# Finer hand placement in a two-layer attention trunk: score steps merged, gates and contraction quarters reordered, key transposes moved

## The chip, the cores and the metric

One core of one Trainium2 chip runs the whole kernel. The metric is the device time of one execution in microseconds (us), compared as the median of several runs. Engines are named as in the profile: PE (TensorE matmul), PEld (its weight loads), DVE (VectorE), ACT (ScalarE), POOL (GpSimd), SP (the queue that issues most DMAs).

## The reference, cut to what matters

Two residual layers work on 256 tokens of width 2048, with a memory of 256 tokens. A head is 128 wide, and all arithmetic is float32.

```
mem_n = rms_norm(mem)
for i in range(2):
    h = rms_norm(x)
    proj = h @ (even_w_in | odd_w_in)                # 2048 x 6680 | 2048 x 6224
    # even: 8 "nsa" heads: compressed + selected-block + window branches, sigmoid gates
    #       4 "diff" heads: softmax_1 - lam * softmax_2, then rms_norm
    #       4 memory heads over mem_n @ mem_w_kv
    # odd : 12 "dsa" heads: an indexer scores the keys, the top 64 of them are attended
    #       4 memory heads
    y = concat(heads) * silu(gate columns of proj)   # 2048 wide: 16 tiles of 128
    x = x + y @ w_out[i]
```

## The kernel before

**Products.** A weight matrix is cut into chunks (the list `CHUNKS`, line 32), and a chunk into pieces of 512 KB or less. Line 174 loads a piece into a ring of four buffers. Lines 185 and 186 split it into a high part `whi` (ACT) and a rest `wlo` (DVE), up to two pieces ahead of the product. Two kinds of product use the pieces. `dense_nat` (line 262) gives tokens by columns in twelve matmuls of 512 columns per piece (24 narrower ones for a narrow chunk). `dense_T` (lines 277 and 278) gives columns by tokens in sixteen matmuls per piece, eight of 512 and eight of 256 columns; it makes the gates (chunks z0 to z7 in the even layer, y0 to y7 in the odd one) and the out projections (o0 to o7, p0 to p7). A gate chunk has four pieces. The products write PSUM tiles named `dn`, of which there are two.

**Order of the chunks.** Keys and values of the memory for both layers (memk0, memv0, memk1, memv1), then the even layer: mq0, cmp0, cmp1, bq, bk, bv, ks, vs0, vs1, aq0, aq1, z0 to z7, o0 to o7; then the odd layer: ikw, iq0, iq1, mq11, ck, cv, cq0 to cq2, y0 to y7, p0 to p7.

**Attention as steps.** Each head is a Python generator; its `yield`s cut it into steps. `attend` (line 211) queues a head. At most two heads are open at once (`lines`), and `step` (line 217) advances them in turn. After each piece, `run_background` lets `PER_PIECE` = 0.9 of a step run; `attended` forces steps until the named heads are over. Steps are traced with high priority. A planner that simulates the engines then sets the order of each engine's queue, so a step may stand later on the chip than where it was traced. Each engine works through its queue in that order.

**Steps of one head.** An nsa head (line 974) has five: scores and softmax of token block 0; the same of block 1; rescaling and the first branch's transposes and split; the second branch's; then the product with the values (lines 1003 to 1005). A diff head (line 842) has four. A dsa head (line 1188) and a memory head (line 543) have three, and both blocks' scores go into one PSUM tile: block 0's matmuls, its softmax, block 1's matmuls, its softmax. Scores, transposes and value products share three PSUM buffers.

**Gate and head meet in `Gated`** (line 422). Each of the 16 tiles of y has two factors. Whichever comes first is stored in `oT` (a head by one ACT copy, line 439; a gate by lines 1029 and 1030), the second is multiplied in (a head by one DVE operation, line 440; a gate by lines 1033 and 1034). When a pair of tiles is complete and its quarter released, `flush` splits it into `y` (lines 286 and 287), which the out projection reads. The quarters hold: 0 and 1 the nsa heads 0 to 3 and 4 to 7, 2 the diff heads, 3 the memory heads; in the odd layer 0 to 2 the dsa heads, 3 the memory heads. A quarter of `y` takes the place of tiles that the heads still read, so the even layer releases 2 and 3 when the diff heads are over and 0 and 1 after all nsa heads; the odd layer releases all four at the end.

**Memory keys.** `mem_k` (line 519) copies memk's product into a tile `nat` (two buffers, shared with its squares), has POOL compute the reciprocal norms by small operations one after the other (`rsq`, lines 301 to 314), multiplies (line 525, DVE), and transposes four heads for each token block on PE (line 354, through the single PSUM buffer `pp`). The transposes are traced right behind the multiplication. While memk0's keys wait for the norms, PE works on memv0 and memk1; for memk1's keys it works on memv1.

Of the kernel before, what the change touches and what calls it, by code (L numbers as in the profile page):

```python
# [33 lines left out]
for _i, _c in enumerate((2584, 2840, 3096, 3352, 5144, 5400, 6168, 6424)):  # L34
    CHUNKS.append((f"z{_i}", "even", _c, 256))
# [5 lines left out]
for _i, _c in enumerate((3664, 3920, 4176, 4432, 4688, 4944, 5712, 5968)):  # L41
    CHUNKS.append((f"y{_i}", "odd", _c, 256))
# [7 lines left out]

OFFS = {}
# [5 lines left out]
NCOLS = {c[0]: c[3] for c in CHUNKS}  # L57

# [57 lines left out]
def trunk(tc, xT, memT, W, w1, w2, consts, ctab, grow, gcol, outT):  # L116
    nc = tc.nc
    V, A, T, G = nc.vector, nc.scalar, nc.tensor, nc.gpsimd
    with ExitStack() as ctx:
# [42 lines left out]
        PER_PIECE = 0.9  # L162
# [88 lines left out]
        def dense_nat(act, name):  # L251
# [4 lines left out]
            for q in range(KT // k):  # L256
                wh, wl = weights(first[name] + q)
                for k_ in range(k):
                    kt = q * k + k_
                    for j, (part, w) in enumerate(((0, wh), (1, wh), (0, wl))):  # L260
                        for tb in range(2):
                            T.matmul(ps[:, tb, :n], act[kt, part, tb * P:(tb + 1) * P], w[:, k_, :],  # L262
                                     start=(kt == 0 and j == 0), stop=(kt == KT - 1 and j == 2), skip_group_check=True)
# [3 lines left out]
        def dense_T(act, name, apart=False):  # L267
# [3 lines left out]
            for q in range(4):  # L271
                wh, wl = weights(first[name] + q)
                for n in range(8):
                    ct, k_ = (n // 4, n % 4) if apart and q == 3 else (n % 2, n // 2)
                    kt = q * 4 + k_
                    cs = slice(ct * P, (ct + 1) * P)
                    T.matmul(ps[:, ct, :], wh[:, k_, cs], act.both(kt), start=(kt == 0), stop=False, skip_group_check=True)  # L277
                    T.matmul(ps[:, ct, S:], wl[:, k_, cs], act[kt, 0, :], start=False, stop=(kt == KT - 1),  # L278
# [143 lines left out]
        class Gated:  # L422
# [3 lines left out]
            def __init__(self, oT, act):  # L426
                self.oT, self.act, self.seen, self.ready, self.free = oT, act, set(), set(), set()

# [90 lines left out]
        def mem_k(v, rm, done):  # L519
# [6 lines left out]
            for tb in range(2):  # L526
                done(tb, transpose4(kn[:, tb], 4, prep_bank()))
# [15 lines left out]
        def mem_attention(q, nsc, qi, h, kT, v, out, obase):  # L543
# [109 lines left out]
        mem_k(dense_nat(memA, "memk1"), rm, spill_k)  # L653
# [55 lines left out]
        out = Gated(big.tile([P, KT, S], F32, name="oT0", tag="S0"), y)  # L709
# [132 lines left out]
        def diff_head(h, q, nsd, bkT, bv, ob):  # L842
            E = tp.tile([P, 2, 3 * P], F32, name="E")
            sm = sp.tile([P, 2, 2], F32, name="sm")
            for tb in range(2):
# [7 lines left out]
                yield  # L853
# [66 lines left out]
        for g in range(2):  # L920
# [3 lines left out]
            if g == 0:  # L924
# [374 lines left out]
```

## Time and profile before

| | us |
|---|---|
| median of 3 runs | 972.97 |
| the runs | 972.97, 973.02, 970.55 |
| the profiled execution | 969.85 |
| its span in the trace | 968.1 |
| PE / PEld / DVE / ACT / POOL busy | 950.3 / 807.5 / 669.6 / 516.8 / 130.1 |

The profiled execution is a run of its own; its span begins with the first instruction and ends with the last. Matmuls are pipelined and their ends are modelled, so PE's busy time runs past the start of the next matmul: 98% busy does not say that PE worked at its full pace, but an idle PE in the trace is idle.

### The profile page before, as it was taken

Reading aid. Unit: us, or ns where it says so; the run is one execution under the profiler, and the core shown is the slowest. Engines: PE = TensorE matmul, PEld = TensorE weight load, DVE = VectorE, ACT = ScalarE, POOL = GpSimd, SP = SyncE. Lnnn points to the kernel's source line nnn. Section 1 sums busy time; section 2 is a strip of 40 time slices with the busy share of each in tenths; the row PEclk is TensorE's granted clock in tenths of the full one; section 3 lists DMA queues with packets and bytes.
Section 4 is the critical chain, followed back from the end, with each engine's and each line's share of the span. In section 5 each row is a group of like instructions: output and inputs, shape, how many; then the busy total and the mean of one; then the engine's idle time right before and its main releaser. Section 6 shows DMA issues by size and latency. Waiting matters only on the chain.

```text
span 968.1 us, 14359 instructions
## 1 busy us (share of the span) xinstructions
PE 950.3 (98%) x5225; PEld 807.5 (83%) x5225; DVE 669.6 (69%) x1137; ACT 516.8 (53%) x853; POOL 130.1 (13%) x345
## 2 busy tenths in 40 slices
PE   8989999999999999999899999999999999999998
PEld 6878788777787888888788898888888888888886
DVE  6768866655665677777776676779766676677553
ACT  6656544545555546666555454555545566564332
POOL 0073120320211220000000131021023020000000
PEclk9999999999999999999999999999999999999999
DMA  9756755757476655344488775544555455546772
GB/s 331 246 194 196 240 187 175 235 188 233 131 264 190 187 168 154 123 140 144 139 257 249 208 236 182 169 132 139 178 187 175 159 170 164 164 131 193 241 236 89
DMA packets 55623, 182.06 MB, mean 188 GB/s; under 512 B 6352, under 2 KB 7888, under 8 KB 55552
## 3 DMA queue, kind: packets, MB, share of 16 engines
q1 hardware_dynamic: 53904, 176.77, 57.4%
q0 software_dynamic: 1216, 4.05, 1.4%
q8 instruction: 41, 0.67, 0.3%
q10 hardware_dynamic: 432, 0.32, 0.1%
q14 instruction: 30, 0.25, 0.1%
HBM read 175.88 MB, written 5.24 MB: 187 GB/s over the span
## 4 chain that ended last, share of the span: by engine, by line
PE 89%; DVE 4%; POOL 2%; DMA 2%; issue 1%; ACT 1%; SPq 0%; ACTq 0%; DVEq 0%; POOLq 0%
PE dn L262 41%; PE dn L277 25%; PE dn L278 13%; DVE wlo L186 1%; PE pp L354 1%; PE S L747 1%; DMA raw<-in_W 1%; PE pt L354 1%; PE S L1131 1%; PE S L983 1%; PE po L1003 1%; PE po L567 1%; ACT whi L185 1%; PE S L550 1%; DMA xs<-in_xT 1%
## 5 line engine op out<-in xcount | busy, mean ns | idle before, releaser
L186 DVE TENSOR_TENSOR wlo<-raw,whi 128x1024 fp32r<-128x1024 f32 (+3 forms) x305 | 364.3, 1196 | 199.3 <-ACT whi L185 196.3
L185 ACT ACTIVATE whi<-raw 128x1024 fp32r<-128x1024 f32 (+3 forms) x305 | 316.5, 1039 | 311.4 <-PE dn L262 129.5
L262 PE MATMUL dn<-whi,h 128*128 128x512 f32 (+3 forms) x1152 | 295.7, 372 | 0.0
L262 PEld LDWEIGHTS dn<-whi,h 128*128 128x128 f32 x1152 | 203.9, 188 | 38.1 <-issue 4.3
L277 PE MATMUL dn<-h,whi 128*128 128x512 f32 x576 | 206.9, 398 | 1.8 <-DVE rp L460 1.8
L277 PE MATMUL dn<-y,whi 128*128 128x512 f32 x512 | 179.7, 397 | 2.2 <-DVE y L287 2.2
L262 PE MATMUL dn<-wlo,h 128*128 128x512 f32 (+3 forms) x576 | 169.5, 373 | 0.0
L278 PE MATMUL dn<-h,wlo 128*128 128x256 f32 x576 | 163.7, 284 | 0.0
L278 PE MATMUL dn<-y,wlo 128*128 128x256 f32 x512 | 142.8, 279 | 0.0
L277 PEld LDWEIGHTS dn<-h,whi 128*128 128x128 f32 x576 | 108.2, 188 | 24.9 <-DVE rp L460 2.2
L262 PEld LDWEIGHTS dn<-wlo,h 128*128 128x128 f32 x576 | 103.4, 188 | 18.6 <-issue 1.6
L277 PEld LDWEIGHTS dn<-y,whi 128*128 128x128 f32 x512 | 96.0, 188 | 25.7 <-DVE y L287 2.7
L278 PEld LDWEIGHTS dn<-h,wlo 128*128 128x128 f32 x576 | 108.8, 189 | 0.7
L278 PEld LDWEIGHTS dn<-y,wlo 128*128 128x128 f32 x512 | 96.4, 188 | 0.1
L262 PE MATMUL dn<-whi,mem 128*128 128x512 f32 x256 | 71.1, 398 | 1.7 <-ACT mem L485 1.2
L262 PEld LDWEIGHTS dn<-whi,mem 128*128 128x128 f32 x256 | 48.5, 191 | 13.7 <-ACT mem L485 2.4
L383 ACT ACTIVATE E<-E,mn 128x128 f32<-128x128 f32 (+1 forms) x88 | 40.2, 457 | 31.3 <-DVE mn L382 24.3
L262 PE MATMUL dn<-wlo,mem 128*128 128x512 f32 x128 | 40.5, 397 | 0.4 <-DVE wlo L186 0.4
L1062 POOL DMA_DIRECT2D x1d<-x x8 | 4.4, 550 | 199.1 <-DVE x L1059 188.1
L262 PEld LDWEIGHTS dn<-wlo,mem 128*128 128x128 f32 x128 | 24.2, 190 | 5.7 <-DVE wlo L186 0.6
L286 ACT ACTIVATE prh<-pt 128x384 fp32r<-128x384 f32 (+2 forms) x36 | 16.8, 473 | 15.2 <-PE pt L354 10.9
L313 POOL TENSOR_SCALAR rsa<-rsa 128x8 f32<-128x8 f32 (+4 forms) x57 | 22.6, 397 | 5.0
(331 smaller groups left out, 967.5 us busy)
## 6 DMA issues: line engine op xcount, KB each, us to landing
raw<-in_W SPq DMA_DIRECT2D x287, 512.0 KB, 3.9
raw<-in_w SPq DMA_DIRECT2D x16, 512.0 KB, 4.4
raw<-in_W SPq DMA_DIRECT2D x8, 336.0 KB, 3.6
raw<-in_W SPq DMA_DIRECT2D x8, 280.0 KB, 3.1
xs<-in_xT SPq DMA_DIRECT2D x8, 256.0 KB, 6.3
ld<-in_xT SPq DMA_DIRECT2D x8, 256.0 KB, 3.6
x1d<-x POOLq DMA_DIRECT2D x8, 256.0 KB, 4.1
ld<-x1d SPq DMA_DIRECT2D x8, 256.0 KB, 3.8
```

The lines of the kernel that those rows point to most:

```text
L185: state["last"] = (A.activation(hi[:, c], r[:, c], AF.Copy), V.tensor_tensor(lo[:, c], r[:, c], hi[:, c].bitcast(F32), OP.subtract))
L186: V.tensor_tensor(lo[:, c], r[:, c], hi[:, c].bitcast(F32), OP.subtract))
L262: T.matmul(ps[:, tb, :n], act[kt, part, tb * P:(tb + 1) * P], w[:, k_, :], start=(kt == 0 and j == 0), stop=(kt == KT - 1 and j == 2), ski ...
L277: T.matmul(ps[:, ct, :], wh[:, k_, cs], act.both(kt), start=(kt == 0), stop=False, skip_group_check=True)
L278: T.matmul(ps[:, ct, S:], wl[:, k_, cs], act[kt, 0, :], start=False, stop=(kt == KT - 1), skip_group_check=True)
L286: A.activation(hi, src, AF.Copy)
L313: G.tensor_scalar(a, a, 1.5, None, OP.add)
L354: T.transpose(ps[:, b, :], src[:, b * P:(b + 1) * P], ident)
L383: A.activation(E, E, AF.Exp, bias=mn, scale=-1.0, accum_out=sm)
L550: T.matmul(ps_s[:, tb, :], a[:, qi, block(tb)], b[:, h, :], start=(j == 0), stop=(j == 2))
L567: T.matmul(po, a[:, mt, h * P:(h + 1) * P], b[:, mt, :], start=(mt == 0 and j == 0), stop=(mt == 1 and j == 2))
L747: T.matmul(ph[l4 * 32:(l4 + 1) * 32, :], blks[j][:, l, :, :].rearrange("p g c -> p (g c)"), wt[:, l4, :], start=(l < 4), stop=(l >= 28), t ...
```

## The change

- Chunks: aq0 goes ahead of vs1. The gates go in the orders `ORDER0` = 3, 2, 1, 0, 4, 5, 6, 7 and `ORDER1` = 5, 4, 3, 0, 1, 2, 6, 7.
- `K_ORDER`: the even layer's out projection contracts the quarters in the order 2, 0, 1, 3; its weights are packed in that order.
- Steps: `PER_PIECE` is 1.2. A diff or nsa head issues the scores of both token blocks in one step (four steps for an nsa head, three for a diff head). A memory head issues both blocks' score matmuls before the first softmax; a dsa head issues block 1's, then block 0's, then the softmaxes in that order.
- A head named in `behind` (even: 2 to 7; odd: 6 to 11) yields ahead of its value product until its gate has been stored.
- `mem_k`'s transposes become a background generator that yields 15 times (memk0) or 5 times (memk1), once per piece, and then queues them behind the last product matmul traced so far.

```diff
-          ("vs0", "even", ((1792, 128), (2304, 128), (2560, 24)), 280), ("vs1", "even", ((1920, 128), (2432, 128)), 256),
-          ("aq0", "even", 0, 512), ("aq1", "even", 512, 512)]
+          ("vs0", "even", ((1792, 128), (2304, 128), (2560, 24)), 280), ("aq0", "even", 0, 512),
+          ("vs1", "even", ((1920, 128), (2432, 128)), 256), ("aq1", "even", 512, 512)]
+ORDER0 = (3, 2, 1, 0, 4, 5, 6, 7)
+ORDER1 = (5, 4, 3, 0, 1, 2, 6, 7)
+K_ORDER = {"out0": (2, 0, 1, 3)}
...
-        PER_PIECE = 0.9
+        PER_PIECE = 1.2
+        MEM_LATER = 15
...
-            for q in range(4):
+            for q, quarter in enumerate(K_ORDER.get(SOURCE[name], range(4))):
...
-                    kt = q * 4 + k_
+                    kt = quarter * 4 + k_
...
+            def waits(self, c):
+
+                return c in self.behind and c not in self.seen
...
-            for tb in range(2):
-                done(tb, transpose4(kn[:, tb], 4, prep_bank()))
+
+            def transposes():
+
+                for _ in range(MEM_LATER):
+                    yield
+                with tc.issue_after(state["product"].ins):
+                    for tb in range(2):
+                        done(tb, transpose4(kn[:, tb], 4, prep_bank()))
+
+            start_background(transposes(), 1)
...
                 for j, (a, b) in enumerate(passes(q, kT)):
                     T.matmul(ps_s[:, tb, :], a[:, qi, block(tb)], b[:, h, :], start=(j == 0), stop=(j == 2))
+            for tb in range(2):
                 softmax_masked(ps_s[:, tb, :], None, nsc[:, tb, qi:qi + 1], E[:, tb, :], sm[:, tb:tb + 1])
...
-        mem_k(dense_nat(memA, "memk1"), rm, spill_k)
+        v = dense_nat(memA, "memk1")
+        MEM_LATER = 5
+        mem_k(v, rm, spill_k)
...
-                yield
+            yield
             V.reciprocal(sm, sm)
             V.tensor_tensor(sm, sm, gate4[:, :, h, 1:3], OP.mult)
...
-            while compressed not in over:
+            while compressed not in over or out.waits(h):
                 yield
...
-        for i in range(8):
+        for i in ORDER0:
             gated(out, f"z{i}", i * 2, h0)
...
+            for j, (a, b) in enumerate(passes(q1, kT)):
+                T.matmul(ps_s[:, 1, :], a[:, qi, :], b[:, g, :], start=(j == 0), stop=(j == 2))
+            T.matmul(ps_s[:, 0, :P], q0[:, qi, :], k0[:, g, :], start=True, stop=True)
+            for tb in (1, 0):
+                softmax_masked(ps_s[:, tb, :(tb + 1) * P], biases[tb], nsc[:, tb, qi:qi + 1], E[:, part(tb)], sm[:, tb:tb + 1])
```

## Rows read from the trace of the kernel before

**Rows 1.** The page: busy time of PE (share of the span, instructions), and the granted clock of PE in 40 equal slices, in tenths.
```profile
PE 950.3 (98%) x5225; PEld 807.5 (83%) x5225; DVE 669.6 (69%) x1137; ACT 516.8 (53%) x853; POOL 130.1 (13%) x345
...
PEclk9999999999999999999999999999999999999999
```

**Rows 2.** The waits of PE's weight loads over the whole span: what waited <- for what: us in total, times, longest.
```profile
PEld pp L354 <- DVE nat L525: 3.1, 1, 3.1
PEld dn L277 <- DVE y L287: 2.7, 2, 1.5
PEld dn L277 <- DVE rp L460: 2.2, 2, 1.3
PEld pt L354 <- DVE prl L287: 2.0, 1, 2.0
...
PEld S L1198 <- DVE mn L382: 1.1, 1, 1.1
...
PEld po L1003 <- DVE prl L287: 0.8, 1, 0.8
```

**Rows 3.** The timeline of PE around 66 us: start, us, instruction, in brackets the idle time before it and what ended it.
```profile
62.49 0.84 PE L262 MATMUL dn<-whi,mem 128*128 128x512 f32 x3
65.99 0.66 PE L354 MATMUL pp<-cst,nat 128*128 128x128 f32 x4 [2.65 <-DVE nat L525]
...
67.29 1.91 PE L262 MATMUL dn<-whi,mem 128*128 128x512 f32 x4
```

**Rows 4.** Two stretches of 20 us: busy us (and instructions) of PE, PEld, DVE, ACT, POOL, then the granted clock, the DMA share and GB/s.
```profile
40.00:60.00 20.00, 20.00 (x94) 16.71 (x93) 14.02 (x25) 10.74 (x16) 7.91 (x21) 1.00 0.82 276
60.00:80.00 20.00, 17.34 (x74) 13.88 (x74) 13.28 (x18) 9.36 (x15) 10.66 (x32) 0.91 0.55 174
```

**Rows 5.** The timeline of POOL, first for memk0's keys (59 to 65 us), then for memk1's (86 to 96 us).
```profile
58.98 0.20 POOL L301 TENSOR_TENSOR ssq<-ssq,rmk 128x8 f32<-128x8 f32 x1
...
64.48 0.20 POOL L301 TENSOR_TENSOR mkf<-mkf,rmk 128x8 f32<-128x8 f32 x1
...
86.30 3.64 POOL L301 TENSOR_TENSOR ssq<-ssq,rmk 128x8 f32<-128x8 f32 x1 [13.27 <-DVE ssq L323]
...
95.84 0.20 POOL L301 TENSOR_TENSOR mkf<-mkf,rmk 128x8 f32<-128x8 f32 x1
```

**Rows 6.** The timeline of all engines around memk1's keys: the copy of the product, DVE work beside POOL, the multiplication, the first transposes.
```profile
81.36 1.01 ACT L522 ACTIVATE nat<-dn 128x1024 f32<-128x1024 f32 x1
...
86.52 1.22 DVE L186 TENSOR_TENSOR wlo<-raw,whi 128x1024 fp32r<-128x1024 f32 x1
...
96.08 1.22 DVE L525 TENSOR_TENSOR nat<-nat,mkf 128x1024 f32<-128x1024 f32 x1 [3.88 <-POOL mkf L301]
...
97.83 0.60 PE L354 MATMUL pp<-cst,nat 128*128 128x128 f32 x4
```

**Rows 7.** The timeline of PE at the end of the even layer's attention. Reading `h` is the last gate, reading `y` the out projection.
```profile
460.80 0.28 PE L278 MATMUL dn<-h,wlo 128*128 128x256 f32 x1
460.92 0.39 PE L277 MATMUL dn<-y,whi 128*128 128x512 f32 x1
...
463.69 1.15 PE L354 MATMUL pt<-cst,E 128*128 128x128 f32 x9
466.61 0.55 PE L354 MATMUL pt<-cst,E 128*128 128x128 f32 x3 [1.77 <-DVE prl L287]
467.68 0.39 PE L1003 MATMUL po<-prh,vv 128*128 128x256 f32 x1 [0.52 <-DVE prl L287]
...
472.22 0.50 PE L277 MATMUL dn<-y,whi 128*128 128x512 f32 x1 [1.28 <-DVE y L287]
```

**Rows 8.** The timeline of PE inside the even layer's gates (389 us) and at the end of the odd layer's attention (858 to 874 us).
```profile
388.90 0.50 PE L277 MATMUL dn<-h,whi 128*128 128x512 f32 x1 [0.72 <-DVE rp L460]
...
858.22 0.62 PE L1198 MATMUL S<-kT,qh 128*128 128x256 f32 x3 [0.86 <-DVE mn L382]
859.96 0.50 PE L277 MATMUL dn<-h,whi 128*128 128x512 f32 x1 [1.11 <-DVE rp L460]
...
874.19 0.50 PE L277 MATMUL dn<-y,whi 128*128 128x512 f32 x1 [0.90 <-DVE y L287]
```

**Rows 9.** The end of the even layer's gates as one stretch, 26 us (columns as in rows 4): all instructions, and below it only those that write or read `dn`.
```profile
435.00:461.00 26.00, 26.00 (x164) 23.21 (x163) 20.39 (x45) 17.91 (x39) 0.00 (x0) 1.00 0.46 142
...
435.00:461.00 26.00, 21.38 (x114) 17.15 (x113) 0.86 (x2) 0.59 (x1) 1.00 0.46 142
```

**Rows 10.** Groups of DVE instructions by line over the span: busy us, mean ns of one | idle before.
```profile
L186 DVE TENSOR_TENSOR wlo<-raw,whi 128x1024 fp32r<-128x1024 f32 (+3 forms) x305 | 364.3, 1196 | 199.3 <-ACT whi L185 196.3 <-PE dn L262 2.2
...
L460 DVE TENSOR_TENSOR rp<-rp,dn 128x512 f32<-128x512 f32 x16 | 10.9, 678 | 0.9 <-ACT rp L459 0.7
L287 DVE TENSOR_TENSOR y<-oT,y 128x512 fp32r<-128x512 f32 x16 | 10.5, 684 | 0.4 <-ACT y L286 0.3
...
L1034 DVE SCALAR_TENSOR_TENSOR oT<-ew,rp 128x512 f32<-128x512 f32 (+1 forms) x12 | 8.0, 664 | 0.2
```

**Rows 11.** Groups of ACT instructions of a gate (columns as in rows 10).
```profile
L1026 ACT ACTIVATE ew<-rp 128x512 f32<-128x512 f32 x16 | 9.9, 621 | 3.7 <-DVE rp L460 3.5 <-DVE rp L1024 0.3
L286 ACT ACTIVATE y<-oT 128x512 fp32r<-128x512 f32 x16 | 9.4, 620 | 2.6 <-PE po L1004 1.5 <-DVE oT L1034 1.0
L459 ACT ACTIVATE rp<-dn 128x512 f32<-128x512 f32 x16 | 9.3, 583 | 1.1 <-DVE oT L1030 1.0
```

More of the change, by code (lines that the diff above doesn't have):

```diff
@@ L57 @@
 NCOLS = {c[0]: c[3] for c in CHUNKS}
+SOURCE = {c[0]: c[1] for c in CHUNKS}
 CC = {}
@@ L261, in dense_nat @@
                         for tb in range(2):
-                            T.matmul(ps[:, tb, :n], act[kt, part, tb * P:(tb + 1) * P], w[:, k_, :],
-                                     start=(kt == 0 and j == 0), stop=(kt == KT - 1 and j == 2), skip_group_check=True)
+                            state["product"] = T.matmul(
+                                ps[:, tb, :n], act[kt, part, tb * P:(tb + 1) * P], w[:, k_, :],
+                                start=(kt == 0 and j == 0), stop=(kt == KT - 1 and j == 2), skip_group_check=True)
                 run_background()
@@ L708, in trunk @@
         y = Act("B", "y0", False)
-        out = Gated(big.tile([P, KT, S], F32, name="oT0", tag="S0"), y)
+        out = Gated(big.tile([P, KT, S], F32, name="oT0", tag="S0"), y, range(2, 8))
         r = region("B", 0, "kT", F32R)
@@ L919, in trunk, with values @@
             split(*[x.rearrange("p g b s -> p (g b) s")[:, :, block(tb)] for x in kT], transpose4(kn[:, tb], 4, prep_bank()))
-        for g in range(2):
+        def values(g):
             w = dense_nat(h0, f"vs{g}")
@@ L1084, in trunk @@
         y = Act("B", "y1", False)
-        out = Gated(big.tile([P, KT, S], F32, name="oT1", tag="S0"), y)
+        out = Gated(big.tile([P, KT, S], F32, name="oT1", tag="S0"), y, range(6, 12))
         r = region("B", 0, "kv1")
@@ L1191, in dsa_head @@
             ps_s = pS.tile([P, 2, S], F32, name="S", tag="one")
-            for tb in range(2):
-                n = (tb + 1) * P
-                if tb == 0:
-                    T.matmul(ps_s[:, 0, :P], q0[:, qi, :], k0[:, g, :], start=True, stop=True)
-                else:
-                    for j, (a, b) in enumerate(passes(q1, kT)):
-                        T.matmul(ps_s[:, 1, :], a[:, qi, :], b[:, g, :], start=(j == 0), stop=(j == 2))
-                softmax_masked(ps_s[:, tb, :n], biases[tb], nsc[:, tb, qi:qi + 1], E[:, part(tb)], sm[:, tb:tb + 1])
+            for j, (a, b) in enumerate(passes(q1, kT)):
[3 more added lines that the diff above has]
+                softmax_masked(ps_s[:, tb, :(tb + 1) * P], biases[tb], nsc[:, tb, qi:qi + 1], E[:, part(tb)], sm[:, tb:tb + 1])
             V.reciprocal(sm, sm)
@@ L1210, in dsa_head @@
             yield
+            while out.waits(h):
+                yield
             vg = slice(g * P, (g + 1) * P)
@@ L1231, in trunk @@
             dsa += [attend(dsa_head(c * 4 + i, q0, q1, nsc), *chosen) for i in range(4)]
-        for i in range(8):
+        for i in ORDER1:
             gated(out, f"y{i}", i * 2, h1, rb1)
```

28 lines of the change are left out of this document (18 added, 10 removed).

## The prediction, made before the changed kernel had run

> **What bounds the kernel now.** I read the page first. PE is busy for 950.3 of 968.1 us at a granted clock of 9 tenths or more in every slice [rows 1]; no other engine passes 69%. Since a busy PE need not be at its pace, the question is how long PE stood still. The waits answer it. Those of the weight loads, which stand at the head of PE's queue, come to 3.1 + 2.7 + 2.2 + 2.0 + 1.1 + 0.8 = 11.9 us in eight waits that belong to lines of the change [rows 2]. The timeline of PE then shows where they lie: one ahead of the transposes of memk0's keys [rows 3], one inside the even layer's gates, three at the end of the even layer's attention [rows 7], and three at the end of the odd layer's [rows 8].
>
> The first costs more than its wait. In the stretch from 60 to 80 us the granted clock is 0.91, and PE starts 74 instructions instead of 94 in the stretch before [rows 4]. The 20 that are missing, at 20/94 = 0.21 us each, are 4.3 us: the wait of 2.65 us and 1.6 us of matmuls at half the clock (1.2 instead of 2.4 GHz). The same shows directly: three matmuls took 0.84 us ahead of the wait, four took 1.91 us behind it [rows 3].
>
> So the most that this change can win is 3.1 + 1.6 for memk0's keys and 11.9 - 3.1 = 8.8 for the others, 13.5 us. It takes no matmul away. Whatever else it does can only move work off or onto PE's waits.
>
> **Memory transposes later.** A background generator yields once per piece, so with 15 yields memk0's transposes are queued at the 16th piece counted from memv0's first: behind memk1's last. Before they stood at 66 us, in memk1's fourth piece, the twelfth in that count [rows 3]; four pieces more at about 2.77 us (a piece of sixteen matmuls runs from 460.92 to 463.69 [rows 7], and one of twelve moves as many columns) give 11 us. The keys are ready at once when DVE's multiplication ends, ahead of 66 us [rows 3], so the wait and the slow matmuls go: **-4.7 us**. Late next on that spot is DVE's `wlo`, queued behind the multiplication that waits for POOL; it works two pieces ahead, 5.5 us, so I price it at 0, at most 0.7.
>
> For memk1's keys the margin is thin. Before, the copy of the product began at 81.36 and the multiplied keys were there at 96.08 + 1.22 = 97.30, 15.9 us later; PE took them at 97.83 without a wait [rows 6]. In the changed kernel the transposes may not stand ahead of the end of memv1's sixth piece, 6 x 2.77 = 16.6 us behind memk1. That alone fits. But `nat` has two buffers: memk1's copy needs the one that memk0's keys leave, and those are now transposed only behind memk1. With one `pp` buffer that takes four transposes (0.66 us [rows 3]), a split on ACT and DVE (0.62 and 0.68, by the split of y [rows 10, 11]), and four more transposes: 2.6 us. The keys are then ready about 18.5 us behind memk1, against 16.6. If the planner foresees it, it places the transposes a piece later and nothing is lost; if not, PE waits 1.9 us, up to the 2.7 us that the reading of 16.7 + 2.6 gives, and pays the slow clock as memk0's did. Behind that copy ACT's `whi` for memv1 is queued; two pieces of lead, 5.5 us, cover 2.6. Between 0 and 2.7 + 1.6 = 4.3 I take **+0.7**, near the row without a wait [rows 6], since the planner placed these keys well before.
>
> POOL is the uncertain part of this chain. The same first operation took 0.20 us for memk0's keys and 3.64 for memk1's, where DVE ran `wlo` beside it [rows 5, 6]; the whole chain took 5.7 us (58.98 to 64.68) and 9.7 us (86.30 to 96.04). The Trainium skill says the same on its page GPSIMD Engine Reference, section 8 (Key points): POOL shares its SBUF interfaces with VectorE, in contention with DVE instructions that have two SBUF inputs. By that rule the later place of memk1's chain is not a safer one, and the thin margin above is a rival, priced below; these rows agree with the rule.
>
> **Steps, merged scores, the pace.** I counted the steps by the code. Before, 0.9 per piece and five steps for an nsa head leave eight steps of heads 6 and 7 undone when the last gate's product ends; PE meets their transposes and value products behind the out projection's first piece, at 463.69, and waits there [rows 7]. With 1.2 per piece and four steps a head takes 3.33 pieces instead of 5.56. Heads 2 and 3 hold both places until z1, the third gate, is stored; the steps in between do nothing, and no engine waits for a generator that yields. Then twenty pieces of gates remain, and the heads 4 to 7 with their compressed branch need (4 x 4 + 2) / 1.2 = 15. The last value product falls to z7's first piece, three pieces (8.3 us) ahead of the gates' end. In the odd layer the heads 8 to 11 need 4 x 3 / 1.2 = 10 of the last twenty pieces. So the transposes and value products that PE waited for (2.0 + 0.8 us), the scores behind a softmax in the same tile (1.1; block 1's matmuls no longer stand behind block 0's softmax), and y of the even layer (1.5 of the 2.7) all go: **-5.4 us**.
>
> The quarters' order gives the out projection one more piece of cover: quarter 2 is ready long before, and quarter 3, which needs the last gate, comes last. That gate's chain is 0.58 + 0.68 + 0.62 + 2 x 0.66 + 0.62 + 0.68 = 4.5 us [rows 10, 11], under the 8.3 us of the three pieces ahead. In the odd layer the order stays 0 to 3; the heads end earlier, so of its wait for y (1.2 us with the load's, 0.90 in rows 8) I let 0.4 stay: **-0.8**. Gates first or heads first changes which engine stores, by some tenths on ACT and DVE, hidden behind PE: 0. aq0 ahead of vs1 moves the same instructions: 0, with one wait as in rows 8 (1.1) as its bound on either side.
>
> **What the denser steps cost.** At the end of the gates, 26 us hold 114 matmuls of products, 7.1 pieces, and 20.39 us of DVE [rows 9]: per piece 3.66 us of time and 2.87 of DVE. Of that `wlo` is 1.20 and a gate's share (0.68 + 2 x 0.66 + 0.68)/4 = 0.67 [rows 10], which leaves 1.00 for the heads; PE's own work for them is 3.66 - 2.77 = 0.89. A head in 3.33 instead of 5.56 pieces makes both 1.67 times as dense: DVE 1.87 + 1.67 = 3.54 us in 2.77 + 1.49 = 4.26, or 83% instead of 78%. It holds on the mean, but bunches can delay a gate's `total` (line 460), for which the product after next waits for its `dn` tile. Such waits were two, 2.2 us together [rows 2, 8]. The old two go where the bunches were (-2.2); for new ones I take **+1.5**, between 0 and 6 (one in every third of the sixteen gates at 1.1).
>
> **The sum.** -4.7 + 0.7 - 5.4 - 0.8 - 2.2 + 1.5 = -10.9 us, say -11. The profiled execution took 969.85 us, of which 968.1 are its span; the median of the runs is 972.97, 3.1 us above it. The waits should be the same in all of them, so I subtract from the median: **962.0 us**. From the profiled execution it would be 958.9.
>
> **Rivals.**
> - *The wait moves to memk1's keys.* For it: the two-buffer `nat`, POOL's 9.7 us. Against it: PE did not wait there before. The price is 4.3 instead of 0.7, so -7.3: 965.7 us. Chance 0.17.
> - *The heads still end behind the gates* (the change doesn't do what it says). Steps are only traced early; the planner and the engines can lag. For it: before, the odd layer's last step was traced in y6, and its scores stood at 858 us, the seventh gate's end [rows 8]. Against it: three pieces of slack in the even layer, nine in the odd. If the even layer's three waits and the odd layer's y stay, 4.3 + 0.8 less is won: -5.9, 967.1 us. Chance 0.13.
> - *Slower: DVE falls behind the gates.* If the denser heads make every gate's `total` late, sixteen gates wait 1.1 us as at 859.96 [rows 8]: +17.6 instead of +1.5, so +5: 978 us. It beats the gain from about eleven gates on. For it: DVE's 83% and its place at the end of most of the waits in rows 2. Against it: only two such waits at 78%. Chance 0.07.
> - *Two of the first two together*: -2.3, 970.7 us. Chance 0.03.
>
> **How the numbers follow.** The forecast has 0.60 and, with the bounds of its terms (no new wait: -13.5, 959.5; six new waits in the gates: -6.4) and the 2.5 us over which the runs scatter, spans 958 to 967. The range 957.5 to 969.5 takes in the first two rivals and leaves out slower and the pair. What counts as no change here is 0.3%, 2.9 us, so faster means below 970.05. That holds for nearly all of the forecast and both first rivals, less the scatter: faster 0.83; same 0.10 (the pair, and rivals meeting a slow set of runs); slower 0.07.
>
> **What would show it.** In the profile after: no wait ahead of `pp` at 63 to 66 us and a granted clock of 1.00 in 60 to 80; memk1's `pp` behind memv1's sixth piece, waiting 0 to 0.7; the last value product of either layer ahead of its last gate's end; no weight load waiting for `prl`; the sum of the listed waits about 2 to 3 us instead of 11.9. The prediction is wrong if PE waits for line 460 in many gates, if memk1's `pp` waits over 2 us with a clock below 1 behind it, or if the out projections' first pieces still wait for y.

## The result and the profile after

The changed kernel takes **958.27 us** (median of four runs, 957.76 to 958.86) beside 972.42 for the kernel before in the same session (four runs, 970.55 to 973.02): ratio 0.9858, 95% interval 0.9841 to 0.9875, or 14.2 us less. The forecast was 962.0 with a range of 957.5 to 969.5, so the time lies inside the range and 3.7 us below the forecast. The profiled execution took 957.76 us, its span 956.0, which is 12.1 us less than the span of before.

I read the page first. PE is as near to the whole span as it was, and its busy time has fallen from 950.3 to 945.0 us with the same 5225 matmuls [rows 1]. Columns as there.

```profile
span 956.0 us, 14345 instructions
PE 945.0 (99%) x5225; PEld 805.8 (84%) x5225; DVE 671.8 (70%) x1138; ACT 515.1 (54%) x850; POOL 130.1 (14%) x345
...
PEclk9999999999999999999999999999999999999999
```

Then the waits of PE's weight loads in the changed kernel: what waited <- for what, us in total, times, longest.

```profile
PEld dn L271 <- DVE wlo L195: 4.0, 4, 2.1
...
PEld pt L529 <- DVE row L527: 1.0, 1, 1.0
```

None of the eight waits of [rows 2] is left. But the wait for `row` is new, and those for `wlo` have grown from 1.4 us in the kernel before:

```profile
PEld dn L262 <- DVE wlo L186: 1.4, 3, 0.6
```

So the forecast's sign of "about 2 to 3 us" of listed waits is missed, with 4.0 + 1.0 = 5.0 us (3.6 without the 1.4 that stood there before). These waits stand in the memory part. Its two stretches, columns as in [rows 4]:

```profile
60.00:80.00 20.00, 17.72 (x79) 14.04 (x79) 13.86 (x21) 9.57 (x15) 10.32 (x30) 1.00 0.57 185
100.00:120.00 20.00, 18.79 (x85) 14.78 (x84) 14.24 (x37) 8.30 (x11) 4.47 (x12) 1.00 0.72 214
```

The clock from 60 to 80 us is 1.00 instead of 0.91, as forecast, and PE still starts only 79 instructions where 94 would fit. The timeline of PE shows where it stands (columns as in [rows 3]):

```profile
66.62 0.73 PE L271 MATMUL dn<-wlo,mem 128*128 128x512 f32 x2 [1.68 <-DVE wlo L195]
...
72.05 0.70 PE L529 MATMUL pt<-row,cst 128*128 128x256 f32 x2 [0.60 <-DVE row L527]
...
78.06 0.60 PE L365 MATMUL pp<-cst,nat 128*128 128x128 f32 x4
...
101.99 0.63 PE L365 MATMUL pp<-cst,nat 128*128 128x128 f32 x4
103.37 0.73 PE L271 MATMUL dn<-wlo,h 128*128 128x512 f32 x2 [0.75 <-DVE wlo L195]
```

memk0's transposes moved from 65.99 to 78.06 and wait for nothing. What is late instead is the low half of the weights. The timeline of DVE in the changed kernel says why:

```profile
64.20 1.23 DVE L541 TENSOR_TENSOR nat<-nat,mkf 128x1024 f32<-128x1024 f32 x1 [2.37 <-POOL mkf L312]
65.35 2.35 DVE L195 TENSOR_TENSOR wlo<-raw,whi 128x1024 fp32r<-128x1024 f32 x2
71.43 0.56 DVE L527 TENSOR_SCALAR row<-cst,rx 128x128 f32<-128x128 f32 x2 [3.73 <-POOL rx L519]
71.83 2.35 DVE L195 TENSOR_TENSOR wlo<-raw,whi 128x1024 fp32r<-128x1024 f32 x2
...
100.62 1.23 DVE L541 TENSOR_TENSOR nat<-nat,mkf 128x1024 f32<-128x1024 f32 x1 [3.87 <-POOL mkf L312]
...
102.10 1.22 DVE L195 TENSOR_TENSOR wlo<-raw,whi 128x1024 fp32r<-128x1024 f32 x1
```

DVE takes its queue in order here: it stood idle for 2.37 us before the multiplication of the keys, which waits for POOL's norms, while a `wlo` was queued behind it whose `whi` ACT had made by 61.44. Two `wlo` come after the multiplication, and PE needs the first of them at 66.62. The same pattern returns at 71 us (`row`, 3.73 us of waiting) and at 100 us (3.87). The transposes were moved; the multiplication ahead of them was not, and DVE's three idle times are those of the kernel before (2.36, 3.73 and 3.88 us there).

At the end of the even layer's gates, where [rows 7] had three waits, the timeline of PE now reads:

```profile
456.14 0.33 PE L1034 MATMUL po<-pcT,ld 96*128 96x256 f32 x1
...
461.37 0.40 PE L287 MATMUL dn<-h,whi 128*128 128x512 f32 x1
...
461.73 0.40 PE L287 MATMUL dn<-y,whi 128*128 128x512 f32 x1
```

The last nsa head's last value product starts at 456.14, 5.6 us ahead of the out projection's first at 461.73. Before, it was at 470.6, behind it. In the odd layer the last value product starts at 838.7 and the out projection at 860.77; before, 870.8 and 874.19 [rows 8].

The starts of the first product of some chunks, found by following the products along PE's timeline, give the account by stage (us, profiled executions):

| stretch | before | after | difference |
|---|---|---|---|
| memory and first projections: memk0 to vs0 | 252.2 | 250.9 | -1.3 |
| even layer's attention and gates: vs0 to o1 | 222.5 | 216.1 | -6.5 |
| out projection: o1 to ikw | 79.1 | 77.7 | -1.4 |
| odd layer's projections: ikw to its first gate | 205.4 | 205.9 | +0.5 |
| odd layer's gates and heads: first gate to p1 | 120.3 | 115.5 | -4.8 |
| out projection: p1 to p7 | 66.6 | 67.8 | +1.2 |
| sum | | | -12.3 |

The differences are taken before rounding.

So the gain is in the two layers' gates, 11.3 us, and hardly in the memory part: -1.3 is inside the scatter of that stage, which took 250.9 to 252.9 us in the five kernels that have all of the changed kernel's code there. Part of the 11.3 us is work that was moved and not saved. Counted in the traces, the two stretches of the gates hold 1337 and 704 matmuls after, 1343 and 710 before; the other six of each are heads' matmuls that now start in the projections ahead, of which the odd ones are 0.5 us longer.

### The profile page after: what moved, and what is told of

It is laid out like the page before. It is cut to its first block, busy times and chain, and to the rows that moved or that the text cites. A ratio compares the mean times of both kernels' runs of the same rounds, so it can differ in the third digit from the quotient of the medians.

```text
span 956.0 us, 14345 instructions
## 1 busy us (share of the span) xinstructions
PE 945.0 (99%) x5225; PEld 805.8 (84%) x5225; DVE 671.8 (70%) x1138; ACT 515.1 (54%) x850; POOL 130.1 (14%) x345
## 4 chain that ended last, share of the span: by engine, by line
PE 91%; POOL 3%; DVE 3%; DMA 2%; issue 1%; SPq 0%; ACT 0%; DVEq 0%; POOLq 0%; ACTq 0%
PE dn L271 40%; PE dn L287 26%; PE dn L289 13%; PE pp L365 1%; PE pt L365 1%; PE S L774 1%; DVE wlo L195 1%; PE S L1012 1%; PE S L1162 1%; PE po L1032 1%; DMA xs<-in_xT 1%; PE po L592 1%; DMA raw<-in_W 1%; PE S L574 1%; DMA ld<-in_grow 1%
## 5 line engine op out<-in xcount | busy, mean ns | idle before, releaser
L394 ACT ACTIVATE E<-E,mn 128x256 f32<-128x256 f32 (+1 forms) x88 | 40.0, 456 | 25.3 <-DVE mn L393 22.9
```

What stands on the lines that cost most here:

```text
L394: A.activation(E, E, AF.Exp, bias=mn, scale=-1.0, accum_out=sm)
```

## The experiments

Two theories stood first. Theory A is the forecast's sum: each part is worth its term, the memory part among them. Theory B: the memory transposes are worth nothing, since a wait of DVE replaces that of PE, and the gain is all in the gates. What in the gates makes it was asked with the later runs. All were timed in five rounds beside the kernel before, whose medians were 972.49, 970.87 and 971.8 us in the three sessions (23, 17 and 17 runs).

**Memory transposes put back in the changed kernel.**

```diff
-            def transposes():
-                for _ in range(MEM_LATER):
-                    yield
-                with tc.issue_after(state["product"].ins):
-                    for tb in range(2):
-                        done(tb, transpose4(kn[:, tb], 4, prep_bank()))
-            start_background(transposes(), 1)
+            for tb in range(2):
+                done(tb, transpose4(kn[:, tb], 4, prep_bank()))
```

> The kernel after with the memory transposes put back where they were; all else as changed. Theory A (the forecast's term): the wait ahead of pp and the slow matmuls behind it come back, so 4.0 us slower than the kernel after (958.3): 962.3 us. Theory B (read from the trace after: DVE's multiplication still waits for POOL and holds back wlo, for which PE then waits 1.8 and 0.8 us): only 0.5 to 2.0 us slower, 958.8 to 960.3 us, with a wait of 2 to 3 us ahead of pp near 63 us and no waits for wlo there.

Measured: 957.57 us (956.55 to 959.02), ratio 0.9843, interval 0.9811 to 0.9876, against 0.9858 for the whole change. Nothing is lost without the moved transposes. The old wait is back in PE's waits (what waited <- for what, total, times, longest), and the new ones are nearly gone:

```profile
PE pp L365 <- DVE nat L541: 2.4, 1, 2.4
...
PE dn L271 <- DVE wlo L195: 0.4, 1, 0.4
```

**Memory transposes alone, in the kernel before.** The same edit the other way round.

> The kernel before with the memory transposes moved as in the change, and nothing else. Theory A: 4.0 us faster than before (972.4): 968.4 us. Theory B: 0.5 to 2.0 us faster, 970.4 to 971.9 us; PE's wait ahead of pp gone, and waits for wlo of about 1.8 and 0.8 us near 66 and 72 us in its place.

Measured: 971.62 us, ratio 1.0004 (0.9978 to 1.003): no change. PE's waits in this kernel show the exchange: 3.1 us for `wlo` (0.4 in the same view of the kernel before) and 0.6 for `row`, where 2.7 for `nat` had stood.

```profile
PE dn L263 <- DVE wlo L187: 3.1, 3, 1.9
```

The starts of the chunks show where the gain goes. Up to mq0's first product the moved transposes do win: it starts at 100.8 us in the changed kernel and at 103.1 with them put back, at 101.0 here and at 103.5 in the kernel before. Then mq0 gives it back, with 24.8 us against 22.2 in the first pair and 24.8 against 22.5 in the second: memk1's transposes now stand in mq0, and so does the wait of 0.75 us at 103.37. Both runs speak for Theory B.

**The multiplication and the norms' broadcast moved later too.** If DVE's order is the cause, work that waits for POOL can be queued further back.

```diff
-            V.tensor_tensor(k3, k3, f[:, :, None].to_broadcast([P, 8, P]), OP.mult)
...
-                for _ in range(MEM_LATER):
+                for _ in range(MEM_LATER - 1):
                     yield
+                with tc.issue_after(state["last"][1].ins):
+                    V.tensor_tensor(k3, k3, f[:, :, None].to_broadcast([P, 8, P]), OP.mult)
+                yield
...
-            rb = bcast_rstd(rx[0])
+            for _ in range(6):
+                yield
+            with tc.issue_after(state["last"][1].ins):
+                rb = bcast_rstd(rx[0])
+            entry[1] = 2.0
...
+        entry = background[-1]
...
-        MEM_LATER = 5
+        MEM_LATER = 7
```

`entry[1] = 2.0` lets the generator that makes `h` take two turns a piece from there on (1.4 before), and 7 moves memk1's transposes two pieces further back.

> The kernel after, but DVE's multiplication of the memory keys is traced with the delayed transposes, one piece ahead of them and behind the last wlo (MEM_LATER 7 for memk1), and the broadcast of the token norms six background turns later, both queued behind wlo. Theory B (DVE's in-order wait for POOL holds back wlo, and that took the place of the wait ahead of pp): PE's waits for wlo near 66, 72 and 103 us (1.8, 0.8 and 1.0 us by the starts of PE's instructions) go: 2.5 to 4 us faster than after, 954.3 to 955.8 us. Rival (POOL's chain itself is late for what follows, so the wait moves on to h or to mq0's product): 0 to 1 us, 957.3 to 958.3 us.

Measured: 961.25 us (959.72 to 962.8), ratio 0.9899 (0.9883 to 0.9914): 3 us slower than the change, which neither theory had. The wait at 66 us is gone, but later ones are longer, by PE's timeline of this kernel:

```profile
73.16 0.70 PE L529 MATMUL pt<-row,cst 128*128 128x256 f32 x2 [1.50 <-DVE row L527]
...
108.44 0.63 PE L365 MATMUL pp<-cst,nat 128*128 128x128 f32 x4 [0.71 <-DVE nat L547]
...
112.57 0.73 PE L271 MATMUL dn<-wlo,h 128*128 128x512 f32 x2 [2.80 <-DVE wlo L195]
```

From mq0's first product to cmp0's passed 28.3 us, against 24.8 in the changed kernel. The wait moves along the chain through POOL; none of the three placements removes it. The run moves several things at once, so it does not say which of them costs the 3 us.

**The pace, taken back in the changed kernel, and alone in the kernel before.**

```diff
-        PER_PIECE = 1.2
+        PER_PIECE = 0.9
```

> The kernel after with 0.9 instead of 1.2 steps per piece. Theory A (the pace with the merged steps is what ends the heads ahead of the gates): with 36 steps for the eight nsa heads and the two compressed branches, and heads 2 and 3 held until the third gate, 20 pieces x 0.9 = 18 steps remain for the 18 that heads 4 to 7 need, so the last value product falls to the last gate's last piece or behind it; the even tail's waits come back in part, +1 to +4 us: 959.3 to 962.3 us. The odd layer needs 12 of 18 steps and stays. Theory C (the order of the gates and quarters alone covers the tail): same as after within 1 us.

Measured: 956.36 us (955.02 to 958.23), ratio 0.9827 (0.9797 to 0.9856). The pace isn't needed: the even layer took 215.2 us from vs0 to o1, against 216.1. The expectation counted four steps for an nsa head; it has three (see below), so the heads 4 to 7 need 4 x 3 + 2 = 14 of the 18 steps, and there is slack at 0.9 too. Its interval overlaps with that of the whole change, so it is not shown to be the better kernel. The kernel before with 1.2 instead of 0.9 is the reverse edit:

> The kernel before with 1.2 instead of 0.9 steps per piece, and nothing else. Theory A (pace is the main cause at both tails): the nsa heads' 44 steps end in z7, so both tails lose most of their waits: 5 to 7 us faster than before, 965.4 to 967.4 us. Theory C (the pace alone bunches the heads, and the merged scores and the gates' order are needed): 0 to 3 us faster, 969.4 to 972.4 us, with new waits for rp L460 inside the gates.

Measured: 973.39 us, ratio 1.0002 (0.9982 to 1.0022). The time stays. By the stages the even layer's gates win 3.1 us (219.4 from vs0 to o1, against 222.5) and the odd layer's lose 7.2 (127.5 from the first gate to p1, against 120.3). This profiled execution has a span of 971.6 us, while that of before, 968.1, is one of the shorter ones of its kernel. PE's waits change kind: those for the late heads give way to one for a head's probabilities in the even layer and to waits for a gate's sum in the odd one.

```profile
PE dn L277 <- DVE rp L460: 5.0, 2, 3.9
PE pt L354 <- DVE E L389: 2.8, 1, 2.8
```

**The quarters in their natural order, in the changed kernel** (`K_ORDER = {}`).

> The kernel after with the even layer's out projection contracting the quarters 0 to 3. The last value product stands 5.6 us ahead of the gates' end in the trace after, so all quarters but the last gate's are ready. Theory F: no change, 957.3 to 959.3 us, no wait for y. Rival (the cover of quarter 2 is needed, because quarters 0 and 1 are split behind the last gate's chain): PE waits 1 to 2.5 us for y at the first piece, 959.3 to 960.8 us.

Measured: 958.73 us (957.46 to 960.75), ratio 0.9878 (0.9859 to 0.9898). No difference to the change that these runs can tell, and the even stretch takes 216.1 us in both.

**The scores as before, in the changed kernel.** One block a step again, for diff and nsa heads, and the old order of scores and softmax in memory and dsa heads. The nsa head's two transposes stay in one step.

```diff
-            for tb in range(2):
                 softmax_masked(ps_s[:, tb, :], None, nsc[:, tb, qi:qi + 1], E[:, tb, :], sm[:, tb:tb + 1])
...
-            yield
+                yield
             V.reciprocal(sm, sm)
...
-            for j, (a, b) in enumerate(passes(q1, kT)):
-                T.matmul(ps_s[:, 1, :], a[:, qi, :], b[:, g, :], start=(j == 0), stop=(j == 2))
-            T.matmul(ps_s[:, 0, :P], q0[:, qi, :], k0[:, g, :], start=True, stop=True)
-            for tb in (1, 0):
-                softmax_masked(ps_s[:, tb, :(tb + 1) * P], biases[tb], nsc[:, tb, qi:qi + 1], E[:, part(tb)], sm[:, tb:tb + 1])
+            for tb in range(2):
+                n = (tb + 1) * P
+                if tb == 0:
+                    T.matmul(ps_s[:, 0, :P], q0[:, qi, :], k0[:, g, :], start=True, stop=True)
+                else:
+                    for j, (a, b) in enumerate(passes(q1, kT)):
+                        T.matmul(ps_s[:, 1, :], a[:, qi, :], b[:, g, :], start=(j == 0), stop=(j == 2))
+                softmax_masked(ps_s[:, tb, :n], biases[tb], nsc[:, tb, qi:qi + 1], E[:, part(tb)], sm[:, tb:tb + 1])
```

> The kernel after with the scores as before: block 0, its softmax, block 1, its softmax, and for nsa and diff heads a step between; pace 1.2, gates and quarters as changed. Theory D (the gates' order with the held heads is what spreads the heads and ends them early; the scores only shorten a chain that has slack): heads 4 to 7 need (4 x 5 + 2)/1.2 = 18.3 of the last 20 pieces, so 0 to 2 us slower than after (958.3): 958.3 to 960.3. Theory E (the merged scores are the cause: without them PE stands behind softmax waits at the tails and the clock falls): 5 to 12 us slower, 963 to 970 us, with waits of S for mn or of pt for E.

Measured: 966.81 us (963.48 to 967.58), ratio 0.9949 (0.9932 to 0.9966): 8 us of the gain are lost, all in the odd layer. The profiled execution is the fastest of the runs, 963.48 us. In it the even layer's stretch is 214.9 us (216.1 after) and the odd layer's gates and heads take 123.9 (115.5 after). The odd layer's last value product falls from 838.7 to 863.2 us, and PE waits there, by the timeline of PE in this kernel:

```profile
861.11 0.49 PE L1247 MATMUL po<-prl,kv 128*128 128x128 f32 x2 [0.78 <-ACT prl L1239]
...
862.65 0.38 PE L1246 MATMUL po<-prh,kI 128*128 128x256 f32 x1 [0.76 <-DVE prh L298]
...
865.76 0.79 PE L287 MATMUL dn<-y,whi 128*128 128x512 f32 x1 [2.32 <-DVE y L298]
```

The stretch of 840 to 880 us (columns as in [rows 4]) has a mean clock of 0.91:

```profile
840.00:880.00 40.00, 36.14 (x202) 31.12 (x201) 27.43 (x47) 21.50 (x39) 0.00 (x0) 0.91 0.40 132
```

**The gates in their old order and no head held, in the changed kernel.**

```diff
-ORDER0 = (3, 2, 1, 0, 4, 5, 6, 7)
-ORDER1 = (5, 4, 3, 0, 1, 2, 6, 7)
+ORDER0 = (0, 1, 2, 3, 4, 5, 6, 7)
+ORDER1 = (0, 1, 2, 3, 4, 5, 6, 7)
...
-                return c in self.behind and c not in self.seen
+                return False
```

> The kernel after with the gates in the orders 0 to 7 and no head waiting for its gate; pace 1.2, merged scores and quarters as changed. Theory D: the heads bunch as with the pace alone (973.4), line 460's waits come back: 4 to 10 us slower than after, 962 to 968 us. Theory E: the merged scores alone end the heads early; without the held heads they end even earlier: -1 to +1 us, 957.3 to 959.3.

Measured: 972.89 us (969.8 to 976.09), ratio 1.0016 (1.0 to 1.0031). The whole gain is gone, more than either theory had, and it goes in the even layer: vs0 to o1 takes 230.8 us, against 216.1. One wait lets the mechanism be read. The timeline of all engines in this kernel:

```profile
448.20 0.33 PE L1034 MATMUL po<-pcT,ld 96*128 96x256 f32 x1
...
448.93 0.36 ACT L455 ACTIVATE oT<-po 128x256 f32<-128x256 f32 x1
...
449.67 0.68 DVE L1064 SCALAR_TENSOR_TENSOR rp<-rp,oT 128x512 f32<-128x512 f32 x1
...
451.42 0.69 DVE L1065 SCALAR_TENSOR_TENSOR oT<-ew,rp 128x512 f32<-128x512 f32 x1
...
451.94 0.63 ACT L297 ACTIVATE memk<-ld 128x512 fp32r<-128x512 f32 x1 [1.70 <-DMA ld<-k1d]
452.48 0.58 ACT L475 ACTIVATE rp<-dn 128x512 f32<-128x512 f32 x1
...
453.21 0.68 DVE L476 TENSOR_TENSOR rp<-rp,dn 128x512 f32<-128x512 f32 x1
...
453.95 0.80 PE L287 MATMUL dn<-h,whi 128*128 128x512 f32 x1 [4.71 <-DVE rp L476]
```

It goes from the head's last value product (448.20) to its copy into `oT` (448.93), the gate's multiplication with it (449.67), the gate's store (451.42 to 452.11), and only then to the next gate's sum (452.48, 453.21), because the gate's tile (`rp1`, one buffer) was taken until the store. That sum frees `dn`, and PE's next product starts after 4.71 us. Where a head is stored first, its gate stands behind it, and behind the gate all dense products but the few for which `dn` has room. The sum is also queued on ACT behind a load of `memk` that landed at 451.94, so in this one place two causes end within 0.4 us of each other.

The count of L1064 says how often this is so: a gate runs it only if its head was stored first. First the group in this kernel (busy us, mean ns | idle before it), then in the changed one:

```profile
L1064 DVE SCALAR_TENSOR_TENSOR rp<-rp,oT 128x512 f32<-128x512 f32 x16 | 11.0, 685 | 2.6 <-ACT oT L455 1.8 <-ACT ew L1057 0.7
```

```profile
L1064 DVE SCALAR_TENSOR_TENSOR rp<-rp,oT 128x512 f32<-128x512 f32 x10 | 6.9, 685 | 0.0
```

All sixteen gates stand behind a head here, ten in the changed kernel, and twelve before, one of them with one of its two tiles only (the last line of [rows 10]).

**Order or hold?** Two runs part them: the changed kernel with `return False` alone, and with the two natural orders alone.

> The changed kernel, but no head is held: a head's value product comes when its own steps are done, whether its gate has been stored or not. The orders of the gates stay. Theory C1 (the hold spreads the heads over the gates; without it they bunch as when both were taken back): 968 to 974 us, even attention 226 to 232, heads bunched with few dense matmuls between them. Theory C2 (the order of the gates is what matters, the hold does nothing more): 956.5 to 960 us, even attention 215 to 217.

> The changed kernel, but the gates go in the order 0 to 7 in both layers; the late heads are still held until their gate is stored. Theory C1 (the hold matters): 956 to 962 us, even attention 215 to 219; in the odd layer the heads 6 to 11 then wait for the fourth to sixth gate, and may end a few us later: 320 to 325. Theory C2 (the order matters): 968 to 974 us, even attention 226 to 232, as when both were taken back.

Measured: the order without the hold 968.47 us (967.57 to 973.49), ratio 0.9971 (0.9955 to 0.9987); the hold without the order 958.44 us (957.58 to 960.25), ratio 0.9868 (0.985 to 0.9885). The hold is the part that works, as Theory C1 had it. Beside it the order of the gates does nothing that these runs can tell (0.9868 beside 0.9858); without it the order is worth about 4 us (968.47 against 972.89, and the two intervals of the ratio do not meet). The stages say the same: the even stretch takes 223.3 us without the hold and 216.2 with it alone, the odd one 119.2 and 114.9. So does the count of gates that stand behind a head: fourteen without the hold, one of them with one tile only, and ten with it alone. Without the hold, the stretch of 406 to 423 us (columns as in [rows 4]) is this:

```profile
406.00:423.00 17.00, 12.30 (x75) 10.60 (x75) 12.65 (x45) 12.16 (x37) 0.00 (x0) 0.90 0.21 63
```

And the timeline of PE around it, in the same kernel:

```profile
405.46 0.28 PE L289 MATMUL dn<-h,wlo 128*128 128x256 f32 x1
...
412.79 0.50 PE L365 MATMUL pt<-cst,E 128*128 128x128 f32 x2 [1.35 <-DVE E L400]
...
418.62 1.26 PE L365 MATMUL pt<-cst,E 128*128 128x128 f32 x6 [1.74 <-DVE E L400]
...
423.19 0.45 PE L287 MATMUL dn<-h,whi 128*128 128x512 f32 x1
```

Between 405.46 and 423.19 no dense product starts. PE has only heads' scores, transposes and value products, and waits at each turn for DVE, which in turn waits for ACT. These two are busy for 12.65 and 12.16 of 17 us: it is a chain from engine to engine with nothing beside it, not a full engine. Why there is nothing beside it, the timelines of ACT and of DVE in this kernel show:

```profile
375.98 0.58 ACT L475 ACTIVATE rp<-dn 128x512 f32<-128x512 f32 x1
...
417.18 0.36 ACT L455 ACTIVATE oT<-po 128x256 f32<-128x256 f32 x1
...
419.67 0.59 ACT L475 ACTIVATE rp<-dn 128x512 f32<-128x512 f32 x1
```

```profile
418.59 0.68 DVE L1065 SCALAR_TENSOR_TENSOR oT<-ew,rp 128x512 f32<-128x512 f32 x1
...
421.11 0.68 DVE L476 TENSOR_TENSOR rp<-rp,dn 128x512 f32<-128x512 f32 x1
```

The sum of gate z2 goes into the gate's tile at 375.98. Its two tiles of y belong to heads 4 and 5, which without the hold were traced ahead of the gate; so it is the gate that multiplies, and it must wait until head 5 is stored at 417.18, 41 us later. The gate's tile is free only after the store at 418.59. By then the products of z1 (its last matmul starts at 389.23) and of z0 (405.46) have filled both `dn`, and z1's sum, at 419.67 and 421.11, is the first that frees one. In the changed kernel z2's gate is stored first, at 378.80. So the mechanism of the run above is also what empties PE of dense products here.

**Fewer parts, put into the kernel before.** First the gates' order and the hold alone, then these with the merged steps.

> The kernel before with one part of the change alone: the gates in the orders 3, 2, 1, 0, 4, 5, 6, 7 and 5, 4, 3, 0, 1, 2, 6, 7, and the late heads held ahead of their value products until their gate is stored. Scores, transposes, pace 0.9, quarters, memory transposes and aq0 stay as before. Theory C (gates' order with held heads, and fewer steps a head, are needed together): held heads of five steps at 0.9 a piece end behind the last gate, so little or nothing is won: 968 to 977 us beside 971 to 973 for before; the last nsa value product after 466 us, with waits for prl and y at the out projection's first pieces. Theory D (the order and the hold alone carry the even layer's gain): 962 to 966 us, the even attention (vs0 to o1) 215 to 217 us instead of 222.5.

> The kernel before with two parts of the change: gates' orders with held heads, and the merged steps (scores of both blocks, and both branches' transposes of an nsa head, in one step). Pace 0.9, quarters, memory transposes and aq0 as before. Theory C: this is the whole gain, 955.5 to 960 us, even attention 215 to 217, odd 320 to 322, a wait for nat of 2 to 3 us ahead of memk0's transposes. Theory D2 (the quarters' order, the pace or aq0 also carry some, hidden in runs that took back one of them alone): 961 to 966 us, with waits for y ahead of the out projections.

Measured: 976.69 us (973.3 to 978.37), ratio 1.0052 (1.0033 to 1.007), for the gates alone, and 965.11 us (963.46 to 966.65), ratio 0.9935 (0.9919 to 0.9951), with the merged steps. Alone, the gates' order and the hold cost 5 us: with five steps a head the held heads end behind the last gate (last nsa value product 475.8 us; 470.6 before). With the merged steps the odd layer has its whole gain (115.0 us from its first gate to p1; 115.5 in the changed kernel), and the even one has none: 223.8 us from vs0 to o1. There PE's waits at the end of the heads are back, by its timeline:

```profile
460.28 0.39 PE L1026 MATMUL po<-prh,vv 128*128 128x256 f32 x1 [1.18 <-DVE prl L298]
...
468.18 0.39 PE L1026 MATMUL po<-prh,vv 128*128 128x256 f32 x1 [0.75 <-ACT prh L297]
...
472.11 0.50 PE L287 MATMUL dn<-y,whi 128*128 128x512 f32 x1 [1.27 <-DVE y L298]
```

My theory of two parts (Theory C) fell with this run. It differs from the changed kernel at pace 0.9 (956.36 us) by the quarters, the memory transposes and aq0's place. The first value products of the nsa heads are at 376.7 us here and 355.1 there, far ahead of any out projection and far behind the memory part, so of the three only aq0's place can have moved them: with aq0 ahead of vs1 they come 21.6 us earlier. All the kernels agree with this. The first score product of the nsa heads with the compressed keys starts at 321.7 to 326.6 us in the nine kernels with aq0 ahead, at either pace, and at 333.8 to 340.1 in the five with aq0 behind. That the earlier start is what restores the even layer's gain is an inference: whether aq0 alone does it, and whether the pace of 1.2 would do it as well, was not run.

## Why the prediction was right, and where it was not

- **The ends of the two layers.** Right in kind: every wait that the sum struck out is gone, and no new one took its place. The listed waits there were 11.9 - 3.1 = 8.8 us [rows 2]; the forecast had 5.4 + 0.8 + 2.2 = 8.4 of gain and 1.5 of loss, so 6.9. The two stretches gave 6.5 + 4.8 = 11.3. The last value products came 5.6 and 22 us ahead of the out projections, where the forecast had 8.3 us and nine pieces (25 us). The term that was too large a loss is "for new ones I take +1.5": in either stretch no wait for line 460's successor is left. The other 2.5 us (11.3 - 8.8) are not in any wait that the profile lists. Part of them is the heads' matmuls that moved out of the two stretches, six in each; I don't know the cause of the rest.
- **The count of steps.** The prediction gives the nsa head four steps. The change also puts both branches' transposes into one step, in a line that the cut of the diff above leaves out:

```diff
                 split(pr[0][:, br, :], pr[1][:, br, :], pt.rearrange("p a b -> p (a b)"))
-                yield
+            yield
```

  So it has three, a head takes 3 / 1.2 = 2.5 pieces, and the heads 4 to 7 need (4 x 3 + 2) / 1.2 = 11.7 pieces instead of 15. The heads were therefore denser than I reckoned, which made the third rival more likely than I thought.
- **"Gates first or heads first changes which engine stores", priced at 0.** This step failed in its reason. Which one is stored first decides whether a gate waits for a head. Without the hold the changed kernel loses 10 us of its 14, and with the old order as well all of it. I took the held heads for a matter of who stores, and they are what kept the third rival (slower, gates late) away. Its mechanism is real: 5.0 us of waiting for a gate's sum in the kernel before with the pace alone, 4.7 in the one without hold and order. But DVE was not full there, as the rival had it (12.65 of 17 us without the hold): the trace has a chain of stores through one buffer. That it is this buffer is read from the traces of two kernels and from the count of L1064; no run gave the tile a second buffer.
- **"aq0 ahead of vs1 moves the same instructions: 0".** Wrong in its reason, by the last run above: its place sets when the heads begin. What that is worth in time was not run by itself. At the pace of 0.9 the parts other than hold and merged steps are together worth 8.7 us (965.11 - 956.36).
- **The memory part, -4.7 + 0.7.** This term was mis-sized: about 0 by both runs (957.57 against 958.27; ratio 1.0004 alone), and -1.3 us by the stage table, inside that stage's scatter. The failing step is "Late next on that spot is DVE's `wlo` ... I price it at 0, at most 0.7". I had seen that `wlo` stands behind the multiplication that waits for POOL and trusted two pieces of lead; DVE stood idle for 2.37 and 3.73 us there, and PE waited 1.68 and 0.60. With the transposes in their old place PE does not wait for `row`; I take it that their own wait had hidden it. The lower clock did go, as forecast, and it is back at 0.91 where the transposes are put back, with no loss of time. memk1's `pp` stands in mq0's first piece and waits for nothing, but `wlo` behind its multiplication costs 0.75. POOL's first operation took 3.25 us there, from 90.90, beside DVE's work, and the same form 0.20 at 100.39, with DVE idle. In the kernel with the multiplication moved later the same first operation ran beside DVE operations of 128x256 and no `wlo` (128x1024), and took 0.31 us, at 93.03.

```profile
90.90 3.25 POOL L312 TENSOR_TENSOR ssq<-ssq,rmk 128x8 f32<-128x8 f32 x1 [18.38 <-DVE ssq L334]
...
100.39 0.20 POOL L312 TENSOR_TENSOR mkf<-mkf,rmk 128x8 f32<-128x8 f32 x1
```

  The Trainium skill's page GPSIMD Engine Reference, section 8 (Key points), says that POOL shares its SBUF interfaces with VectorE, in contention with DVE instructions of two SBUF inputs; these rows agree.
- **The quarters: "one more piece of cover".** Not needed in the changed kernel (958.73 without it), since the heads end ahead of the gates.
- **The clock.** The forecast subtracted the waits of a profiled execution from a median that was 3.1 us above it. Spans fell by 12.1 us and medians by 14.2. In the 57 later runs of the kernel before the median granted clock was 0.996, in the four of the changed kernel 0.998. By the line below that is 1.5 us of the difference. That fewer waits make fewer falls of the clock is my reading; no run shows it apart.

The sum came out near by luck, because two errors cancelled: 4 us too much in the memory part, 4.4 too little in the gates (11.3 - 6.9).

## What to carry to other kernels

When the consumer of a late result is moved away, ask what else is queued behind the instruction that waits for it: if that engine works in order, the next consumer is late instead. Where two producers write one tile in either order, the one that goes second waits for the first: make the one that everything else queues behind go first. Take parts back one by one and also together, since parts that are worth nothing singly can stand in for each other.

## What the runs showed of the hardware

The scatter of this kernel goes with the granted clock. In 57 runs of the kernel before, the 18 with a mean granted clock of 0.998 took 968.8 to 972.1 us, the six at 0.992 took 973.2 to 975.9, and the four at 0.989 to 0.991 took 974.0 to 979.0. A line by least squares through all 57 is 968.4 us at full clock and 7.5 us more for each 0.01 below it.

The out projections have two paces, whatever was edited. The 28 pieces from o1 to ikw took 79.1 us in the kernel before and with the hold alone, and 77.7 in the changed kernel; the 24 from p1 to p7 took 66.6 before and 67.8 after. That is 2.83 or 2.78 us a piece, at a full granted clock and with no wait listed. Of the fourteen kernels, five had the slower pace in the first projection and five in the second, and only one of them in both. It makes the -1.4 and +1.2 of the stage table, and no run tells what selects it.
